# RG-LRU gates as 64x64 blocks on four array quadrants in one-bank pieces, the modulation's steps summed outside PSUM, and the keys' latent transposes ahead of the last chunk's scans

## The chip, the cores and the metric

The kernel runs on one core of one Trainium2 chip. The metric is the time of one execution in microseconds (us) as the device measures it; less is better. PE is the matrix engine (TensorE), PEld its loading of weights, DVE the vector engine, ACT the scalar engine, POOL the general-purpose engine (GpSimd), and SP the engine on whose queue all the DMAs of this kernel are issued.

## The reference, cut to what matters

The kernel computes one layer with a token mixer and a gated ConvFFN, on 1024 latent tokens and 256 context tokens of width 1024. The change touches one part of the token mixer, the RG-LRU group: 512 channels in 8 heads of 64.

```python
xr, gr, cq, ckv, kr = split_in_proj(h @ w_in)          # h: tokens, 1024 wide
xc = dwconv(xr, conv_w, conv_b, left=2)                # 4 taps
for d, reverse in ((0, False), (1, True)):             # two directions
    xh = xc.reshape(bsz, n, 8, 64)
    r = sigmoid(einsum('blhi,hij->blhj', xh, w_a[d]).reshape(bsz, n, 512) + b_a[d])
    i = sigmoid(einsum('blhi,hij->blhj', xh, w_x[d]).reshape(bsz, n, 512) + b_x[d])
    log_a = -8.0 * r * softplus(-lam[d])
    a = exp(log_a)
    u = sqrt(-expm1(2 * log_a)) * (i * xc)
    h[d] = linear_scan(a, u, h0, reverse)              # latent tokens start from the context's state
y_lru = (h[0] + h[1]) * gelu(gr)
kv = rms_norm(ckv, g_kv) @ w_ukv                       # keys and values of the attention group
```

Also in this stage is the rest of the modulation: silu(c) and silu(c_ctx) times w_mod plus b_mod gives shifts, scales and gates for later parts of the layer; some of them are worked out here.

## The kernel before

The kernel is one program whose stages follow each other. The change lies in the stage of the in-projection of the RG-LRU columns (lines 398 to 681). A loop at L656 goes over eight projections, m = 0 to 7, each 128 output channels from 1024 inputs. The first four (m < 4) are the RG-LRU's inputs over 1280 tokens (1024 latent, 256 context), in chunks of 512, 512 and 256 columns; the last four are the gate branch (Gelu) over the latent tokens alone. Each is done in split precision: weights and tokens are parted in a high and a low half (`split`, whose low half is the subtraction at L76; L69 is the copy for the high half), and three products are summed in PSUM (L492, L494, L496).

Around the projections stand three kinds of other work. "Chunk m" below is the RG-LRU work on 128 channels (two heads).

- The **modulation steps** (`mod2_step`): 16 steps of four matmuls, each on 32 of the array's columns. Four steps build up one result, which selection matmuls (L433, or L436 for the last two results) then add over groups of rows. Their weights come by DMA into two R pages per step, each step's load being issued one step ahead.
- **Conv and gates**: `conv` (L527) writes the convolved channels into a page `xc[m]`; `gate` (L540) multiplies them with a block-diagonal 128x128 matrix (two heads' 64x64 blocks, zeros elsewhere), three matmuls per gate into a three-bank PSUM tile, then one sigmoid of 1280 columns. Each chunk has four gates (two directions, r and i).
- **Coefficients and scans**: `coefs` (L558) does Exp, Tanh on ACT and a product on DVE; `scans` (L571) does Sqrt on ACT, then on DVE a multiply-add (L578), a product (L579), four scans (L581 to L587) and the sum of both directions (L591).

After projections 1, 2, 3 and 5 follow the gates, coefficients and scans of chunks 0, 1, 2 and 3. After projection 5 the tokens' other columns are also normed (`tok_norm`); `ckv_t` (L631) transposes the keys' latent part (L637) and evicts it (L642), and after projection 6 the keys' weights are loaded and split (wkh, wkl). The first matmuls that use these halves stand at L713 and L714, in the stage behind.

PSUM has here a pool with two tags: "big", two buffers of three banks (projections and gates), and "sm", two buffers of one bank (modulation steps, transposes of the keys). In SBUF the R pool has 12 pages of 128x1280, for conv, gates, coefficients and the modulation's weights; a W pool has 5 pages for weights, an L pool 30 pages. A page that is used again makes the next user wait for the last reader. A scheduler sets the order of each engine's instructions from the program's; each engine then runs its list strictly in that order, and SP issues the DMAs strictly in its order too.

Of the kernel before, what the change touches and what calls it, by code (L numbers as in the profile page):

```python
# [34 lines left out]
def hybrid_layer_kernel(ctx: ExitStack, tc: tile.TileContext, A, out):  # L35
# [20 lines left out]
    def R(dt=F32, shape=(128, 1280)):  # L56
        cnt[0] += 1
        return rp.tile(list(shape), dt, tag="R", name=f"r{cnt[0]}")
# [354 lines left out]
    def mod2_step(s):  # L413

        n, kp = divmod(s, 4)
        if s + 1 < 16:
            mod2_load(s + 1)
        if kp == 0:
            acc2[n] = ps_small()
        ws_ = w2.pop(s)  # L420
        for j in range(2):
            for h in range(2):
                g = 64 * h + 32 * j
                T.matmul(acc2[n][g:g + 32, :], cs[:, 2 * kp + j, :], ws_[j][:, h * 512:(h + 1) * 512], start=kp == 0, stop=kp == 3,
                         tile_position=(0, g))
        if kp == 3:
            mr = R()
            S.activation(mr[:, 0:512], acc2.pop(n), AF.Copy)
            po = ps_small()
            if n < 2:  # L430
                pt = po[:, 0:8].rearrange("p (m h) -> p m h", h=2)
                for m in range(4):
                    T.matmul(pt[:, m, :], mr[:, m * 128:(m + 1) * 128], sel2, start=True, stop=True)  # L433
                V.tensor_copy(mod2[:, n].rearrange("p (h m) -> p m h", h=2), pt)
            else:
                T.matmul(po[0:2, :], sel2, mr[:, 0:512], start=True, stop=True)  # L436
                r = 2 * (n - 2)
                rw, gr = (mr[0:2, 512 + 256 * x:768 + 256 * x] for x in range(2))
                for h in range(2):
                    c = slice(h * 256, (h + 1) * 256)  # L440
                    for x, q_ in ((rw, r), (gr, r + 1)):
                        nc.sync.dma_start(out=x, in_=A["rows"][q_:q_ + 1, :].rearrange("o (a b) -> (o a) b", a=2)[:, c])
                    V.tensor_tensor(rw, po[0:2, c], rw, ALU.add)
                    V.tensor_tensor(rw, rw, gr, ALU.mult)
                    nc.sync.dma_start(out=gt_d[n - 2:n - 1, :].rearrange("o (a b) -> (o a) b", a=2)[:, c], in_=rw)
# [72 lines left out]
    wg = {}  # L518

    def load_wg(m):  # L520
        wg[m] = L(F32, (128, 4, 128))
        nc.sync.dma_start(out=wg[m], in_=A["wg"][:, m * 512:(m + 1) * 512].rearrange("p (i n) -> p i n", i=4))

    SEG = ((0, SEQ), (SEQ, CTX))
    xc = {}

    def conv(m, po):  # L527

# [8 lines left out]
                V.scalar_tensor_tensor(out=x[:, a:b], in0=xr[:, a + d:b + d], scalar=cw[k], in1=x[:, a:b],  # L537
                                       op0=ALU.mult, op1=ALU.add)

    def gate(m, d, g):  # L540
        po = ps1.tile([128, 1536], F32, tag="big", name=f"pg{m}{d}{g}", bufs=2)
        for a, n in CH3:
            T.matmul(po[:, a:a + n], wg[m][:, d * 2 + g, :], xc[m][:, a:a + n], start=True, stop=True)
        r = R()
        S.activation(r, po[:, 0:NTOK], AF.Sigmoid, bias=P("bx" if g else "ba", d * 4 + m, 1))
        return r

    ysum = {}

# [3 lines left out]
        V.tensor_tensor(ysum[m], ysum[m], g[:, :SEQ], ALU.mult)  # L553

    def gates(m):
        return [(gate(m, d, 0), gate(m, d, 1)) for d in range(2)]

    def coefs(m, ri):  # L558

# [87 lines left out]
    def ps_small():  # L647
        cnt[0] += 1
        return ps1.tile([128, 512], F32, tag="sm", name=f"pm{cnt[0]}", bufs=2)
# [8 lines left out]
    for n, m in enumerate(order):  # L658
# [12 lines left out]
        if m in after:  # L671
            au = coefs(after[m], gates(after[m]))
            if m == 5:
                tok_norm()
            scans(after[m], au)
        if m == 6:
            ckv_t()
            raw = load_w(A["w_ukv"])
            wkh, wkl = prep_w(raw, "a", "v")
    pe_ctx.close()  # L680
# [1068 lines left out]
```

## Time and profile before

| what | value |
|---|---|
| time, median of 3 runs | 1319.72 us (1319.44 to 1320.05) |
| profiled execution, its own time | 1321.15 us |
| its span in the trace | 1319.3 us |
| mean granted PE clock | 0.988 of full speed |
| PE busy | 1273.5 us, 97% |
| PEld busy | 1049.8 us, 80% |
| DVE busy | 1019.7 us, 77% |
| ACT busy | 733.3 us, 56% |
| POOL busy | 410.3 us, 31% |

The busy times are shares of the span, over all stages. All times inside the trace count from the span's start. Which engine sets the time of one stage is read from that stage's own window, not from these shares.

### The profile page before, as it was taken

How to read it: one execution, taken by the hardware profiler on the slowest of the kernel's cores; microseconds unless marked ns; L12 is line 12 of the kernel's file. 1: busy time of each engine (PE TensorE's matmuls, PEld its weight loads, DVE VectorE, ACT ScalarE, POOL GpSimd, SP SyncE). 2: the span in 40 equal slices, each digit the busy share in tenths (PEclk: the TensorE clock that was granted, in tenths of full speed). 3: DMA queues.
4: the chain of work that ended last, by engine and by line, in shares of the span. 5: the costliest groups of instructions: out<-in, count | busy, mean ns of one | idle time of the engine just before them, and what ended most of it. 6: DMA issues, size and time to landing. Idle time of an engine off the chain costs nothing.

```text
span 1319.3 us, 17942 instructions
## 1 busy us (share of the span) xinstructions
PE 1273.5 (97%) x6490; PEld 1049.8 (80%) x6490; DVE 1019.7 (77%) x1654; ACT 733.3 (56%) x1374; POOL 410.3 (31%) x378
## 2 busy tenths in 40 slices
PE   5999999799999999999997999999999999999997
PEld 3796666687999999888875888888888888888885
DVE  4653676767898989857589888878777878887797
ACT  3543785557999999954265344433433444434581
POOL 2410000224666666733024433343244330000013
PEclk8999999899999999999999999999999999999998
DMA  9533234000000000243321222221222149204043
GB/s 371 201 116 128 88 127 137 24 1 1 1 1 2 1 1 24 91 159 112 128 97 55 104 81 96 96 80 64 96 96 80 64 140 356 95 0 175 1 144 127
DMA packets 41319, 124.20 MB, mean 94 GB/s; under 512 B 4600, under 2 KB 4880, under 8 KB 41232
## 3 DMA queue, kind: packets, MB, share of 16 engines
q1 hardware_dynamic: 41232, 123.07, 26.4%
q8 instruction: 51, 0.84, 0.3%
q14 instruction: 36, 0.29, 0.1%
HBM read 101.02 MB, written 22.03 MB: 93 GB/s over the span
## 4 chain that ended last, share of the span: by engine, by line
PE 80%; DVE 11%; ACT 5%; issue 2%; DMA 2%; SPq 0%; POOL 0%; DVEq 0%; ACTq 0%; POOLq 0%
PE b L1217 10%; PE b L1215 10%; PE b L1216 10%; PE t L914 5%; PE po L1063 4%; PE b L1392 4%; PE b L1391 4%; PE b L1393 4%; DVE l L76 3%; PE s L878 3%; PE o L939 3%; PE o L938 3%; PE s L879 3%; PE s L880 2%; PE po L1066 2%
## 5 line engine op out<-in xcount | busy, mean ns | idle before, releaser
L1217 PE MATMUL b<-l,f 128*128 128x512 f32 x620 | 242.6, 391 | 5.6 <-DVE f L76 5.6
L1216 PE MATMUL b<-l,f 128*128 128x512 f32 x620 | 242.9, 392 | 3.9 <-DVE l L76 3.8
L1215 PE MATMUL b<-l,f 128*128 128x512 f32 x620 | 242.4, 391 | 0.5 <-issue 0.5
L1216 PEld LDWEIGHTS b<-l,f 128*128 128x128 f32 x620 | 116.9, 189 | 30.7 <-DVE l L76 6.4
L1217 PEld LDWEIGHTS b<-l,f 128*128 128x128 f32 x620 | 117.0, 189 | 30.5 <-DVE f L76 6.4
L1215 PEld LDWEIGHTS b<-l,f 128*128 128x128 f32 x620 | 117.0, 189 | 25.1 <-issue 0.7
L1190 ACT ACTIVATE f<-w 128x1024 fp32r<-128x1024 f32 x21 | 22.3, 1060 | 198.8 <-POOL w L1187 198.8
L906 POOL TENSOR_SCALAR r<-r,c 128x512 f32<-128x512 f32 (+1 forms) x128 | 100.8, 800 | 97.3 <-DVE c L901 68.4
L883 DVE TENSOR_REDUCE c<-s 128x1 f32<-128x512 f32 (+1 forms) x192 | 108.8, 595 | 25.5 <-PE s L880 24.1
L76 DVE TENSOR_TENSOR f<-w,f 128x1024 fp32r<-128x1024 f32 (+1 forms) x90 | 98.4, 1095 | 33.8 <-ACT f L1190 32.8
L1274 DVE SCALAR_TENSOR_TENSOR l<-f,c,l 128x1023 f32<-128x1023 f32 x88 | 122.5, 1393 | 0.7
L894 ACT ACTIVATE r<-s,c 128x512 f32<-128x512 f32 (+1 forms) x192 | 117.5, 620 | 6.3 <-DVE c L901 4.8
L1184 POOL TENSOR_TENSOR w<-w 128x512 f32<-128x512 f32 x21 | 27.9, 1328 | 230.7 <-DVE f L76 230.7
L76 DVE TENSOR_TENSOR l<-t,l 128x512 fp32r<-128x512 f32 x128 | 81.5, 679 | 1.5 <-ACT l L69 1.3
L914 PE MATMUL t<-c,r 128*128 128x128 f32 x640 | 81.7, 273 | 0.9 <-DVE r L76 0.6
L1614 POOL TENSOR_TENSOR f<-f,w 128x1024 f32<-128x1024 f32 (+1 forms) x5 | 11.7, 2372 | 202.7 <-ACT l L1580 202.7
L69 ACT ACTIVATE l<-t 128x512 fp32r<-128x512 f32 x128 | 69.4, 595 | 8.5 <-PE t L914 7.7
L1268 ACT ACTIVATE l<-f,c 128x1024 f32<-128x1024 f32 x44 | 54.5, 1238 | 35.0 <-DVE f L1255 34.4
L914 PEld LDWEIGHTS t<-c,r 128*128 128x128 f32 x640 | 71.2, 140 | 2.6 <-PE t L914 0.8
L878 PE MATMUL s<-r,w 96*128 96x512 f32 (+1 forms) x192 | 69.5, 362 | 1.0 <-ACT r L894 0.7
L1063 PE MATMUL po<-l,r 128*128 128x512 f32 x256 | 69.3, 390 | 0.0
L879 PE MATMUL s<-r,w 96*128 96x512 f32 (+1 forms) x192 | 68.6, 357 | 0.0
(349 smaller groups left out, 3221.5 us busy)
## 6 DMA issues: line engine op xcount, KB each, us to landing
w<-in_w_up SPq DMA_DIRECT2D x44, 512.0 KB
r<-in_w_mod SPq DMA_DIRECT2D x32, 512.0 KB
act<-l SPq DMA_DIRECT2D x22, 512.0 KB
l<-in_w_m SPq DMA_DIRECT2D x16, 512.0 KB
l<-act SPq DMA_DIRECT2D x27, 256.0 KB
l<-in_w_dn SPq DMA_DIRECT2D x27, 256.0 KB
w<-in_w_fm SPq DMA_DIRECT2D x8, 512.0 KB
w<-in_w_out SPq DMA_DIRECT2D x8, 512.0 KB
```

The source lines that it names most:

```text
L76: return (V if e == "v" else G).tensor_tensor(o, src, f(hi), ALU.subtract)
L878: T.matmul(ps[:, :n], qh[0:96, q], kh[0:96, a:a + n], start=True, stop=False)
L879: T.matmul(ps[:, :n], qh[0:96, q], kl[0:96, a:a + n], start=False, stop=False)
L883: V.tensor_reduce(out=stat[:, i % 4, c:c + 1], in_=sc[i, c][:, :CK[c][1]], op=ALU.min, axis=AX.X)
L894: S.activation(pt_[i][:, a:a + n], sc.pop((i, c))[:, :n], AF.Exp, scale=-1.0, bias=st[:, 3:4], accum_out=st[:, 4 + c:5 + c])
L906: G.tensor_scalar(out=p[:, a:a + n], in0=p[:, a:a + n], scalar1=stat[:, i % 4, 7:8], scalar2=1.0, op0=ALU.mult, op1=ALU.mult)
L914: T.transpose(ps[:, c, :], pt_[i][:, (c0 + c) * 128:(c0 + c + 1) * 128], ident)
L1063: T.matmul(po[:, n * 512:(n + 1) * 512], w, wo[k][0][:, n * 512:(n + 1) * 512], start=st, stop=en)
L1215: T.matmul(po, wh, bh, start=k == 0 and b == wb[0][1], stop=False)
L1216: T.matmul(po, wh, bl, start=False, stop=False)
L1217: T.matmul(po, wl, bh, start=False, stop=k == 3 and b == wb[-1][1])
L1274: V.scalar_tensor_tensor(out=x[:, a], in0=x0[:, b], scalar=P("fcw", j * 3 + k, 1), in1=x[:, a], op0=ALU.mult, op1=ALU.add)
```

## The change

The gates become 64x64 blocks. `load_wg` loads only the two blocks of each gate, in four small DMAs, and lays them so that one direction's second gate has its halves swapped. `conv` also makes `xcs[m]`, a copy of the convolved channels with the two halves of partitions exchanged, by two DMAs from SBUF to SBUF. `gate_pair` takes both gates of a direction at once: for each chunk of 512, 512 and 256 columns, a **slot** of four 64x64 matmuls, one on each quadrant of the array, writes two one-bank "sm" tiles, and each is followed by a sigmoid of that chunk. So a sigmoid of 1280 columns becomes three, of 512, 512 and 256 columns, and the gates no longer use the "big" tiles.

`mod2_step` no longer sums four steps in one bank: each step takes a bank of its own, and DVE copies it into (first step) or adds it to an R page; the copy by ACT at the end goes. And `ckv_t` stands ahead of the last chunk's scans in the program.

```diff
--- before.py
+++ after.py
@@ -415,17 +415,20 @@
         n, kp = divmod(s, 4)
         if s + 1 < 16:
             mod2_load(s + 1)
-        if kp == 0:
-            acc2[n] = ps_small()
+        pm = ps_small()
         ws_ = w2.pop(s)
         for j in range(2):
             for h in range(2):
                 g = 64 * h + 32 * j
-                T.matmul(acc2[n][g:g + 32, :], cs[:, 2 * kp + j, :], ws_[j][:, h * 512:(h + 1) * 512], start=kp == 0, stop=kp == 3,
+                T.matmul(pm[g:g + 32, :], cs[:, 2 * kp + j, :], ws_[j][:, h * 512:(h + 1) * 512], start=True, stop=True,
                          tile_position=(0, g))
+        if kp == 0:
+            acc2[n] = R()
+            V.tensor_copy(acc2[n][:, 0:512], pm)
+        else:
+            V.tensor_tensor(acc2[n][:, 0:512], pm, acc2[n][:, 0:512], ALU.add)
         if kp == 3:
-            mr = R()
-            S.activation(mr[:, 0:512], acc2.pop(n), AF.Copy)
+            mr = acc2.pop(n)
             po = ps_small()
             if n < 2:
                 pt = po[:, 0:8].rearrange("p (m h) -> p m h", h=2)
@@ -518,11 +521,16 @@
     wg = {}
 
     def load_wg(m):
-        wg[m] = L(F32, (128, 4, 128))
-        nc.sync.dma_start(out=wg[m], in_=A["wg"][:, m * 512:(m + 1) * 512].rearrange("p (i n) -> p i n", i=4))
+
+        wg[m] = L(F32, (128, 2, 2, 64))
+        src = A["wg"][:, m * 512:(m + 1) * 512].rearrange("p (d g n) -> p d g n", d=2, g=2)
+        for g in range(2):
+            for b in range(2):
+                p = b ^ g
+                nc.sync.dma_start(out=wg[m][64 * p:64 * p + 64, :, g, :], in_=src[64 * b:64 * b + 64, :, g, 64 * b:64 * b + 64])
 
     SEG = ((0, SEQ), (SEQ, CTX))
-    xc = {}
+    xc, xcs = {}, {}
 
     def conv(m, po):
 
@@ -537,13 +545,23 @@
                 V.scalar_tensor_tensor(out=x[:, a:b], in0=xr[:, a + d:b + d], scalar=cw[k], in1=x[:, a:b],
                                        op0=ALU.mult, op1=ALU.add)
 
-    def gate(m, d, g):
-        po = ps1.tile([128, 1536], F32, tag="big", name=f"pg{m}{d}{g}", bufs=2)
+        y = xcs[m] = R()
+        for p in (0, 64):
+            nc.sync.dma_start(out=y[64 - p:128 - p, :], in_=x[p:p + 64, :])
+
+    def gate_pair(m, d):
+
+        ri = R(), R()
         for a, n in CH3:
-            T.matmul(po[:, a:a + n], wg[m][:, d * 2 + g, :], xc[m][:, a:a + n], start=True, stop=True)
-        r = R()
-        S.activation(r, po[:, 0:NTOK], AF.Sigmoid, bias=P("bx" if g else "ba", d * 4 + m, 1))
-        return r
+            po = [ps_small() for g in range(2)]
+            for h in (0, 64):
+                for g in range(2):
+                    o = h ^ (64 * g)
+                    T.matmul(po[g][o:o + 64, 0:n], wg[m][h:h + 64, d, g, :], (xcs if g else xc)[m][h:h + 64, a:a + n], start=True,
+                             stop=True, tile_position=(h, o))
+            for g in range(2):
+                S.activation(ri[g][:, a:a + n], po[g][:, 0:n], AF.Sigmoid, bias=P("bx" if g else "ba", d * 4 + m, 1))
+        return ri
 
     ysum = {}
 
@@ -553,7 +571,7 @@
         V.tensor_tensor(ysum[m], ysum[m], g[:, :SEQ], ALU.mult)
 
     def gates(m):
-        return [(gate(m, d, 0), gate(m, d, 1)) for d in range(2)]
+        return [gate_pair(m, d) for d in range(2)]
 
     def coefs(m, ri):
 
@@ -672,9 +690,9 @@
             au = coefs(after[m], gates(after[m]))
             if m == 5:
                 tok_norm()
+                ckv_t()
             scans(after[m], au)
         if m == 6:
-            ckv_t()
             raw = load_w(A["w_ukv"])
             wkh, wkl = prep_w(raw, "a", "v")
     pe_ctx.close()
```

Line numbers of the changed file differ: its steps' matmuls are L423, the selections L436 and L439, the gates' matmuls L560, their sigmoids L563, Exp L583, Tanh L584, Sqrt L591, the scans L599 to L605.

How the order of instructions moves is shown at three places.

**PE, the end of chunk 1's gates.** Names: pg and pm are PSUM tiles, pf a projection; r, l, w, c are pages of the pools, with their numbers. Before, the gates of chunk 1 (L543) stand among steps of the modulation (L424) and a selection (L433):

```order
L543 MATMUL pg_1277<-r_1100,l_1097 128x512
L433 MATMUL pm_1250<-c_84,r_1248 128x2 x4
L424 MATMUL pm_1260<-r_1240,c_77 32x512 x2
L424 MATMUL pm_1260<-r_1241,c_77 32x512 x2
L543 MATMUL pg_1277<-r_1100,l_1097 128x512
L543 MATMUL pg_1277<-r_1100,l_1097 128x256
L424 MATMUL pm_1260<-r_1256,c_77 32x512
L543 MATMUL pg_1283<-r_1100,l_1097 128x512 x2
L543 MATMUL pg_1283<-r_1100,l_1097 128x256
L424 MATMUL pm_1260<-r_1256,c_77 32x512
```

After:

```order
L560 MATMUL pm_1381<-r_1119,l_1113 64x256
L560 MATMUL pm_1382<-r_1128,l_1113 64x256
L560 MATMUL pm_1381<-r_1119,l_1113 64x256
L560 MATMUL pm_1382<-r_1128,l_1113 64x256
L423 MATMUL pm_1492<-r_1308,c_77 32x512 x2
L423 MATMUL pm_1492<-r_1309,c_77 32x512 x2
L423 MATMUL pm_1502<-r_1488,c_77 32x512 x2
L423 MATMUL pm_1502<-r_1489,c_77 32x512 x2
L423 MATMUL pm_1512<-r_1498,c_77 32x512 x2
L423 MATMUL pm_1512<-r_1499,c_77 32x512 x2
L439 MATMUL pm_1518<-r_1317,c_84 2x512
L560 MATMUL pm_1550<-r_1325,l_1319 64x512 x2
```

The last slot of chunk 1 is now followed by three whole steps, 9, 10 and 11, with nothing between them, then by the selection matmul that uses their sum and the first slot of chunk 2; projection 5 (pf_1699) comes after these.

**ACT, the same place.** Before, the four sigmoids of chunk 1 stand together, then the Exps and Tanhs of both directions:

```order
L545 ACT_TABLE_LOAD
L545 ACTIVATE r_1281<-pg_1277,c_70 128x1280
L545 ACTIVATE r_1287<-pg_1283,c_70 128x1280
L545 ACTIVATE r_1293<-pg_1289,c_70 128x1280
L545 ACTIVATE r_1299<-pg_1295,c_70 128x1280
L565 ACT_TABLE_LOAD
L565 ACTIVATE r_1301<-r_1281,c_851 128x1280
L565 ACTIVATE r_1305<-r_1293,c_851 128x1280
L566 ACTIVATE r_1281<-r_1281,c_852 128x1280
L566 ACTIVATE r_1293<-r_1293,c_852 128x1280
L573 ACT_TABLE_LOAD
```

After:

```order
L563 ACTIVATE r_1363<-pm_1365,c_70 128x512
L563 ACTIVATE r_1364<-pm_1366,c_70 128x512
L583 ACT_TABLE_LOAD
L583 ACTIVATE r_1389<-r_1337,c_851 128x1280
L563 ACT_TABLE_LOAD
L563 ACTIVATE r_1363<-pm_1373,c_70 128x512
L563 ACTIVATE r_1364<-pm_1374,c_70 128x512
L584 ACTIVATE r_1337<-r_1337,c_852 128x1280
L563 ACTIVATE r_1363<-pm_1381,c_70 128x256
L591 ACT_TABLE_LOAD
L591 ACTIVATE r_1337<-r_1337 128x1280
L563 ACT_TABLE_LOAD
```

The sigmoids of one direction (pages 1363 and 1364) now stand among the Exp, Tanh and Sqrt of the other (1389, 1337), with a table load at each change of function.

**SP, the loads for steps 10 and 11.** Names: w is a page for a projection's weights, r a page for the modulation's weights; the brackets list what the issue waits for (DMAHW are earlier DMAs, the others engines; the number behind a page is its buffer). Before:

```order
L411 DMA r218_1400<-in_w_mod 128x1024
L411 DMA r219_1401<-in_w_mod 128x1024 [waits DMAHW7_49,DMAHW2_49,PE_49]
L411 DMA r220_1408<-in_w_mod 128x1024 [waits DMAHW3_49,DMAHW0_49,PE_49]
L411 DMA r221_1409<-in_w_mod 128x1024 [waits DMAHW1_49,Activation_49]
L411 DMA r222_1416<-in_w_mod 128x1024 [waits DVE_49,PE_49]
L411 DMA r223_1417<-in_w_mod 128x1024 [waits DVE_49]
L442 DMA r224_1424<-in_rows 2x256 [waits DMAHW6_49,DMAHW4_49,PE_49]
L442 DMA r224_1424<-in_rows 2x256 [waits DMAHW5_49]
```

After:

```order
L480 DMA w287_1673<-in_w_fm 128x1024 [waits DMAHW5_49,DVE_49]
L550 DMA r229_1334<-r228_1325 64x1280 [waits DMAHW6_49,DVE_49]
L550 DMA r229_1334<-r228_1325 64x1280 [waits DMAHW7_49]
L480 DMA w298_1752<-in_w_fm 128x1024 [waits DMAHW5_49,DMAHW0_49,DVE_49]
L411 DMA r252_1488<-in_w_mod 128x1024 [waits DMAHW1_49,PE_49]
L411 DMA r253_1489<-in_w_mod 128x1024 [waits DMAHW2_49,PE_49]
L411 DMA r255_1498<-in_w_mod 128x1024 [waits DMAHW3_49,DVE_49,Activation_49]
L411 DMA r256_1499<-in_w_mod 128x1024 [waits DMAHW4_49,DVE_49]
L411 DMA r258_1508<-in_w_mod 128x1024 [waits DVE_49,Activation_49]
L411 DMA r259_1509<-in_w_mod 128x1024 [waits DMAHW6_49,DMAHW1_49,PE_49]
```

After the change the load of projection weights w287 waits for DVE, namely for a weight split (L76); behind it stand the two swap copies (r229 from r228, L550). Pages r252 and r253 (step 10) wait for PE's step 9, r255 and r256 (step 11) for DVE's work on chunk 1.

## Rows read from the trace of the kernel before

**Rows 1.** Page part 1: busy us, share of the span, instructions.

```profile
PE 1273.5 (97%) x6490; PEld 1049.8 (80%) x6490; DVE 1019.7 (77%) x1654; ACT 733.3 (56%) x1374; POOL 410.3 (31%) x378
```

**Rows 2.** Windows: start:end, length; PE, PEld, DVE, ACT, POOL busy; PEclk, DMA share, GB/s.

```profile
90.80:252.00 161.20, 160.75 (x733) 107.52 (x731) 100.53 (x129) 94.60 (x85) 8.74 (x5) 1.00 0.34 116
...
259.00:264.40 5.40, 5.40 (x22) 4.92 (x23) 4.61 (x6) 2.70 (x3) 0.00 (x0) 0.50 0.00 0
...
300.00:1319.00 1019.00, 996.23 (x5128) 846.71 (x5127) 832.27 (x1357) 572.21 (x1141) 367.24 (x331) 0.99 0.24 83
```

**Rows 3.** PE's waits, 80 to 320 us: us in total, times, longest.

```profile
PE ck L637 <- DVE l L642: 6.9, 1, 6.9
...
PE pm L424 <- DMA r<-in_w_mod: 0.5, 1, 0.5
```

**Rows 4.** PE's timeline: start, us, engine, line, operation, out<-in, count, [idle before].

```profile
90.77 0.75 PE L492 MATMUL pf<-l,w 128*128 128x512 f32 x3
...
104.94 2.78 PE L424 MATMUL pm<-r,c 128*32 128x512 f32 x24
...
132.41 4.56 PE L543 MATMUL pg<-r,l 128*128 128x512 f32 x12
...
191.84 0.81 PE L492 MATMUL pf<-l,w 128*128 128x512 f32 x2
...
203.03 1.90 PE L424 MATMUL pm<-r,c 128*32 128x512 f32 x10
205.39 1.05 PE L424 MATMUL pm<-r,c 128*32 128x512 f32 x4 [0.45 <-DMA r<-in_w_mod]
...
263.35 0.63 PE L714 MATMUL pb<-w,l 128*128 128x512 f32 x1
```

**Rows 5.** ACT's timeline, 147 to 184 us, columns as in rows 4.

```profile
152.13 0.60 ACT L428 ACTIVATE r<-pm 128x512 f32<-128x512 f32 x1 [0.57 <-PE pm L424]
...
155.41 1.28 ACT L545 ACT_TABLE_LOAD   x1
156.71 1.33 ACT L545 ACTIVATE r<-pg,c 128x1280 f32<-128x1280 f32 x1
...
167.85 2.62 ACT L565 ACTIVATE r<-r,c 128x1280 f32<-128x1280 f32 x2
...
178.68 1.06 ACT L69 ACTIVATE w<-w 128x1024 fp32r<-128x1024 f32 x1 [1.96 <-PE pf L494]
```

**Rows 6.** DVE's timeline, three stretches between 147 and 312 us.

```profile
147.40 2.89 DVE L578 SCALAR_TENSOR_TENSOR r<-r,r 128x1280 f32<-128x1280 f32 x2 [7.53 <-ACT r L573]
...
156.44 2.33 DVE L587 TENSOR_TENSOR_SCAN r<-r,r 128x1024 f32<-128x1024 f32 x1
...
240.23 2.89 DVE L578 SCALAR_TENSOR_TENSOR r<-r,r 128x1280 f32<-128x1280 f32 x2 [7.54 <-ACT r L573]
...
259.49 1.21 DVE L76 TENSOR_TENSOR w<-w,w 128x1024 fp32r<-128x1024 f32 x1
...
308.12 1.27 DVE L76 TENSOR_TENSOR l<-t,l 128x512 fp32r<-128x512 f32 x2
```

**Rows 7.** SP's queue, 216 to 222 us: one issue of a weight load.

```profile
217.15 0.35 SPq L477 DMA_DIRECT2D w<-in_w_fm  x1
```

**Rows 8.** Windows around that load, columns as in rows 2.

```profile
217.10:218.00 0.90, 0.90 (x11) 0.25 (x13) 0.87 (x6) 0.00 (x0) 0.00 (x0) 1.00 0.00 0
218.00:218.50 0.50, 0.50 (x12) 0.20 (x8) 0.43 (x3) 0.00 (x0) 0.00 (x0) 1.00 1.01 180
...
220.00:220.50 0.50, 0.50 (x3) 0.09 (x2) 0.00 (x0) 0.50 (x2) 0.00 (x0) 1.00 0.13 49
```

**Rows 9.** POOL's timeline, 243 to 253 us.

```profile
243.33 1.88 POOL L73 TENSOR_SCALAR l<-l 128x768 fp32r<-128x768 f32 x1 [71.03 <-PE pf L494]
...
249.52 2.08 POOL L76 TENSOR_TENSOR l<-l,l 128x768 fp32r<-128x768 f32 x1
```

## The prediction

> **What bounds the kernel now.** The page comes first: PE is busy for 1273.5 of 1319.3 us [rows 1]. The change lies in the stage of the in-projection, so I cut that stage out by windows: from 90.8 to 252.0 us PE is busy for 160.75 of 161.2 us, DVE for 100.53 and ACT for 94.60 [rows 2]. PE's own work is the length of this stage; DVE and ACT have a third to spare. The list of PE's waits adds one: 6.9 us before the transposes of the keys' latent part (L637), for DVE, which works on the last chunk's scans [rows 3]. Afterwards PE has half its clock (granted 0.50, that is 1.2 GHz) until 264.4 [rows 2]. From 300 us on PE is busy for 996 of 1019 us [rows 2], so whatever delays the first matmul that needs the low half of the keys' weights (L714, at 263.35 [rows 4]) goes to the end whole. I compare that point.
>
> **The change by its sums.** Two gates take six matmuls, 12 records, in 4.56 us [rows 4], so sixteen take 36. Now a slot is four 64x64 matmuls on four quadrants. No row shows row halves of the array at work together, but a step of the modulation is four matmuls on column quarters, and three such steps take 2.78 us [rows 4]: 0.95 for a slot of 512 columns, 0.5 for 256, 4.8 for a chunk, 19.2 for all four, if halves overlap as quarters do. The other bound, halves that take turns, doubles this (a rival below); I take the overlap, as the row of quarters is nearest. Half a step, two matmuls, costs 1.05 us [rows 4], as much as a whole one; so every step or slot that the order cuts in two pays twice. By the changed order of PE's instructions six of the 16 steps are cut (5.7), and about ten slots (some 7.7). PE's own gain is then 36 - 19.2 - 7.7 - 5.7, about 3 us.
>
> DVE gets 16 evictions of a bank, each near 0.68 (a subtraction of 128x512 out of PSUM, two in 1.27 [rows 6]): 11 us. ACT loses four copies of 0.60 and gets sigmoids in pieces: 512 columns near 0.60, 256 near 0.36, worked out between the copy's 0.60 and 1.33 for 1280 columns [rows 5]; 8 pairs cost 3.12 instead of 2.66, together 3.7 more. The changed order also holds 15 more table loads (37 against 22), 1.28 each [rows 5]: 19 us. The eight swap copies of conv's output go by DMA; they only queue on SP. By these sums nothing overflows: ACT 115, DVE 112, PE near 158. But a gate has only two banks now, and ACT must empty both before the next slot starts; so the order decides, and I walked it: each instruction gets its row's duration and starts when what it waits for is done.
>
> **The walk.** Up to the end of projection 4 there is enough projection work between the gates. Five projections (14.17 with context, 104.94 - 90.77; 11.19 without, 203.03 - 191.84 [rows 4]), nine steps, five of them cut, chunk 0's gates and chunk 1's first slot make 91 us, with 4.5 of waits: 186. Before, that projection ended at 203.0 [rows 4], with fewer gates left. Now PE has left: three projections 33.6, gates 13.45 plus 5.8 for cut slots, seven steps and a cut 7.6, two sums 1.9, transposes 1.1: 63.4, to 249.4 if it never waited. The waits:
>
> 1. Chunk 1's other five slots, with no projection between them. ACT first has to copy weights (1.06 [rows 5]) that SP may load only after DVE's weight split, which stands behind chunk 0's scans; the split ends at 187.4 in the walk. A load takes 3.1 us from issue to last byte (issued at 217.15 [rows 7]; its bytes move until just past 220 [rows 8]); ACT is free at 191.5. Then each slot is 0.95 of PE and a pair of sigmoids (1.15) in turn, and the last stands behind two table loads and an Exp (3.9 [rows 5]). PE is through at 201.6: 15.6 us for 3.85 of work, 11.75 lost.
> 2. Steps 9 to 11 of the modulation and their sum. Step 10's weights go into step 9's pages, so their load waits for step 9: 3.1 us, and 1.1 for the second. Step 11's pages come free with two DVE operations of chunk 1 (208.0 and 209.35), then 3.1 again. The sum waits for an addition that stands on DVE behind the multiply that waits for Sqrt (213.1). PE is through at 216.2: 14.6 for 3.8, 10.8 lost.
> 3. Projection 5: 1.5 lost at one slot, whose bank DVE empties late.
> 4. Chunk 2's other slots, with four short pieces of projection: 229.6 to 241.0 for 6.75 of work, 4.65 lost.
> 5. Steps 12 to 14: two more loads that wait for the step before; and projection 6 needs projection 4's banks, which ACT empties by a Gelu that stands behind four table loads, with an Exp, a Sqrt and a Tanh. 241.0 to 252.35 for 2.85, 8.5 lost.
> 6. Projections 6 and 7 with chunk 3's slots: 1.5 lost.
>
> Together 38.7, so PE ends the projections near 288, against 252.
>
> **The tail.** The transposes now stand ahead of the last scans, and their wait of 6.9 us goes. But on DVE the split of the keys' weights (L76) still stands behind these scans. The first Sqrt of chunk 3 ends at 286.7 in the walk. From the first multiply to the last scan's end DVE took 11.4 us in chunk 0 (147.40 to 156.44 + 2.33 [rows 6]); with a product, the sum of directions and the split, 1.13 each when queued (1.21 alone [rows 6]), that makes 14.8: 301.5. In the last chunk of before the scans, product and sum with two evictions of the keys' part took 4.3 us longer, 19.26 from 240.23 to 259.49 [rows 6] against 15.0 by these prices, while POOL split the queries' weights (243.33 to 251.6 [rows 9]). In the change that load waits for the last projection, so POOL's work meets the scans again, partly: between 0 and 4.3, I take 2.2. The low half is then ready at 303.7; before, its first use was at 263.35. **The sum is 40.3 us later.** The half clock after the wait is paid in both. Made against the profiled 1321.15 us this is 1361.4; against the median of the runs, 1319.72, it is 1360.
>
> **The rivals.**
>
> The walk holds: 1360, chance 0.68.
>
> Row halves take turns. Both halves of a gate write the same bank, in different partitions. A slot is then 1.9: 19.2 more, of which some 2 vanish in waits: 1377. For it: no row has row halves. Against it: column quarters, which also share one bank, do overlap [rows 4]. Chance 0.12. The Trainium skill, TensorEngine Tiling (Array Packing), section Restrictions and Gotchas, states this as a rule: different row tiles cannot access one PSUM bank at the same time. By that rule the four quadrants would give two at a time and the time would be 1377; no run here shows it yet.
>
> The loads and pages cost less than I gave them: if pages come free earlier, half of waits 2 and 5 goes (10 us), and POOL misses the scans (2): 1348. For it: before, PE waited 0.5 us in all for such loads [rows 3]; against: there the next pages were not the last step's. Chance 0.11.
>
> Faster: the slots hide behind projection work after all and PE never waits. Then PE ends at 249.4, but the tail still follows the last gates: 303.7 - 38.7 = 265, 1.6 later than before, 1321. It is faster only if cut slots cost nothing either (5.8): 1315. The point that decides: less than 4 of the 38.7 us of waits may remain. For it: ACT, DVE and PE all fit by their sums. Against: three stretches where the order puts nothing between slots or steps. Chance 0.06 (faster), and 0.03 for no change, where the waits left just eat the gain.
>
> **How the numbers follow.** 1360 is the likeliest. The range goes down past the third rival to 1342, since savings at several waits can add, and up to 1378 for the second. A change under 0.2% (2.6 us) can't be told from none. Faster 0.06, same 0.03, slower 0.91.
>
> **What would show it.** In the new trace PE's idle time between 180 and 300 should be near 40 us in three or four clumps: before gate matmuls (L560) for ACT's sigmoids (L563), before steps (L423) for loads of the modulation weights, before the sum (L439) for DVE. Table loads: 15 more. The first use of the keys' low half should come near 303, and the rest of the kernel should be as long as before. The prediction is wrong if PE stays busy through the gates, or if a slot of four takes about 1.9 us when nothing is waited for.

## The result, and the profile after

The changed kernel takes 1373.75 us (median of 4 runs, 1371.06 to 1373.80) beside 1319.88 for the kernel before in the same runs: ratio 1.0400, 95% interval 1.0382 to 1.0418, so 53.9 us slower. The prediction was 1360, with a range of 1342 to 1378. The profiled execution took 1373.77 us, with a span of 1372.0.

The page's first part, of the changed kernel (busy us, share, instructions; before: [rows 1]):

```profile
PE 1294.7 (94%) x6586; PEld 1040.0 (76%) x6586; DVE 1024.9 (75%) x1670; ACT 757.7 (55%) x1417; POOL 408.5 (30%) x378
```

PE is busy for 21 us more although the gates' matmuls do half the columns; that needs an explanation, and so do the 31 us of the longer span that are no PE work. The stage by windows (columns as in [rows 2]):

```profile
91.00:184.00 93.00, 91.29 (x458) 58.53 (x458) 39.23 (x68) 39.17 (x44) 0.64 (x1) 1.00 0.37 118
184.00:262.00 78.00, 54.54 (x213) 20.02 (x211) 39.47 (x39) 48.94 (x52) 0.00 (x0) 0.76 0.34 106
262.00:301.50 39.50, 37.57 (x166) 20.92 (x164) 24.44 (x37) 28.39 (x32) 5.33 (x4) 1.00 0.15 48
...
320.00:1372.00 1052.00, 1027.38 (x5311) 875.02 (x5309) 854.78 (x1398) 592.32 (x1182) 374.74 (x340) 0.99 0.23 81
```

Up to 184 us PE is nearly always busy, as before. From 184 to 262 it is idle for 23.5 of 78 us, and its granted clock is 0.76 on average, where before it was 1.00 in this stage. Behind 320 us nothing has changed: 1027 of 1052 us busy. From 180 to 300 us PE is idle for 25.4 us, where the prediction looked for some 40. The list of PE's waits from 80 to 345 us, its first six rows (us in total, times, longest; before: [rows 3]):

```profile
PE pm L560 <- ACT r L563: 15.6, 9, 5.2
PE pb L732 <- DVE w L76: 8.7, 1, 8.7
PE pm L423 <- DMA r<-in_w_mod: 7.3, 5, 4.2
PE pb L717 <- ACT r L570: 2.2, 1, 2.2
PE pm L423 <- ACT r L563: 1.5, 2, 1.0
PE pm L439 <- DVE r L429: 1.3, 2, 0.8
```

The clumps are those of the walk: gates for ACT's sigmoids, steps for loads, the sum (L439) for DVE, and at the end the first use of the keys' low half (L732) for DVE's split. The swap copies are not in the list: no matmul is seen to wait for one. PE's timeline in the same kernel, slots and steps picked out:

```profile
137.57 1.07 PE L560 MATMUL pm<-r,l 64*64 64x512 f32 x2
...
148.40 1.09 PE L560 MATMUL pm<-r,l 64*64 64x512 f32 x8
...
189.91 1.09 PE L560 MATMUL pm<-r,l 64*64 64x512 f32 x8
...
196.21 4.16 PE L560 MATMUL pm<-r,l 64*64 64x256 f32 x16 [5.20 <-ACT r L563]
...
206.41 1.70 PE L560 MATMUL pm<-r,l 64*64 64x256 f32 x8 [3.59 <-ACT r L563]
...
214.81 3.07 PE L423 MATMUL pm<-r,c 128*32 128x512 f32 x8 [4.24 <-DMA r<-in_w_mod]
...
220.77 1.92 PE L423 MATMUL pm<-r,c 128*32 128x512 f32 x4 [0.66 <-DMA r<-in_w_mod]
223.49 1.87 PE L439 MATMUL pm<-r,c 128*2 128x512 f32 x2 [0.79 <-DVE r L429]
...
314.99 0.80 PE L732 MATMUL pb<-w,l 128*128 128x512 f32 x1 [8.68 <-DVE w L76]
```

At 137.57 one matmul of a slot stands alone (2 records, 1.07 us), at 148.40 four on their four quadrants take 1.09. At 206.41 a slot of 256 columns takes 1.70, at 159.98 (full clock) it took 0.83; half a step (two matmuls, 4 records), 1.05 in [rows 4], takes 1.92 at 220.77. These are the same operations at the lower of the two clocks (granted 0.50), which stands behind the waits of 5.20, 3.59 and 4.24 us. The low half's first use is at 314.99, 51.6 us later than in [rows 4].

### The profile page after: what moved, and what is told of

It reads as the page before. It is cut to its first block, busy times and chain, and to the rows that moved or that the text cites. A ratio compares the mean times of both kernels' runs of the same rounds, so it can differ in the third digit from the quotient of the medians.

```text
span 1372.0 us, 18241 instructions
## 1 busy us (share of the span) xinstructions
PE 1294.7 (94%) x6586; PEld 1040.0 (76%) x6586; DVE 1024.9 (75%) x1670; ACT 757.7 (55%) x1417; POOL 408.5 (30%) x378
## 4 chain that ended last, share of the span: by engine, by line
PE 78%; DVE 11%; ACT 6%; issue 2%; DMA 2%; SPq 0%; POOL 0%; DVEq 0%; ACTq 0%; POOLq 0%
PE b L1235 9%; PE b L1233 9%; PE b L1234 9%; PE t L932 4%; PE po L1081 4%; PE b L1410 4%; PE b L1411 4%; PE b L1409 4%; DVE l L76 3%; PE s L896 3%; PE o L957 2%; PE o L956 2%; PE s L897 2%; PE s L898 2%; PE po L1084 2%
## 5 line engine op out<-in xcount | busy, mean ns | idle before, releaser
L76 DVE TENSOR_TENSOR f<-w,f 128x1024 fp32r<-128x1024 f32 (+1 forms) x90 | 98.3, 1094 | 34.6 <-ACT f L1208 33.6
L76 DVE TENSOR_TENSOR l<-t,l 128x512 fp32r<-128x512 f32 x128 | 81.5, 678 | 1.5 <-ACT l L69 1.3
L896 PE MATMUL s<-r,w 96*128 96x512 f32 (+1 forms) x192 | 69.6, 362 | 1.0 <-ACT r L912 0.7
L956 PE MATMUL o<-l,r 128*128 128x256 f32 x256 | 68.7, 301 | 0.0
```

The source lines that it names most:

```text
L76: return (V if e == "v" else G).tensor_tensor(o, src, f(hi), ALU.subtract)
L896: T.matmul(ps[:, :n], qh[0:96, q], kh[0:96, a:a + n], start=True, stop=False)
L956: T.matmul(OT[j], v, hi, start=(c == 0), stop=False)
```

## The experiments

All times are medians beside the kernel before, which took 1319.8 to 1321.1 us in these runs.

### Parts of the change alone

**Only the steps** (mod2_step as in the change's diff; gates and transposes as before).

> Of the changed kernel only the steps: each modulation step takes a bank of its own and DVE adds it into an R page; gates (128x128, one sigmoid each) and the place of the keys' transposes as before. Theory (the gates' two banks set the order): PE's work is the same, DVE gets 16 evictions of 0.68 us in a stage where it is idle for 60 us, so 1318 to 1324, PE still busy through 90 to 252. Rival (the steps' pages and evictions cost most of the 54 us): 1345 or more, with PE waiting for loads of the modulation's weights by 10 us and more.

1333.94 us, ratio 1.0105 (1.0088 to 1.0122). Neither theory's number. The loads cost little; the sum does. Its waits, and the DVE operation that ends the longest one:

```profile
PE pm L436 <- DVE r L429: 5.0, 1, 5.0
PE pm L439 <- DVE r L429: 2.8, 2, 2.6
...
PE pm L423 <- DMA r<-in_w_mod: 1.2, 1, 1.2
```

```profile
158.28 2.32 DVE L590 TENSOR_TENSOR_SCAN r<-r,r 128x1024 f32<-128x1024 f32 x1
160.53 0.66 DVE L429 TENSOR_TENSOR r<-pm,r 128x512 f32<-128x512 f32 x1
```

Before, the four steps were summed in PSUM and ACT's copy stood alone between the last step and the selection. Now the last addition (L429) stands on DVE behind the scans of chunk 0 (L590), and PE waits 5.0 us; the same once more, 2.6. PE's waits up to the low half's first use are 8.6 us longer than before, its work 3.6 us (168.6 against 165.0, the clock of the stage being 0.95 on average): together the 12.5 us by which that use comes later, within 0.3. DVE's 16 evictions fit into its idle time, but not at the place where they stand.

**Gates and steps without the moved transposes.**

```diff
             if m == 5:
                 tok_norm()
-                ckv_t()
             scans(after[m], au)
         if m == 6:
+            ckv_t()
             raw = load_w(A["w_ukv"])
```

> The changed kernel with the keys' transposes back behind projection 6, as before. Theory: the transposes' place is worth only what their wait was, and the low half of the keys' weights comes behind the scans in both; 1373 to 1380, best guess 1376. Rival (the move itself costs, since it puts three PSUM pieces into the two banks that the last gates use): faster than the changed kernel by 3 us and more, below 1370.

1373.96 us, ratio 1.0406 (1.0390 to 1.0421): the move is worth nothing here. The low half of the keys' weights comes behind the scans in both, so the wait has only another name (L655 for DVE, 14.0 us, in place of L732).

### Table loads

`last_sig` is the chunk's last sigmoid; what stands under it is issued behind it.

```diff
+            with tc.issue_after(last_sig[0].ins):
                 S.activation(a, r, AF.Exp, scale=n8[:, c])
                 S.activation(r, r, AF.Tanh, scale=p4[:, c])
```

> The changed kernel, but each chunk's Exp and Tanh are issued only after that chunk's last sigmoid, so the stage has 15 table loads fewer on ACT (19 us of ACT's time). Theory (a slot waits for two banks whatever stands between; and what follows Exp, Tanh and Sqrt comes later): 1366 to 1376, best guess 1371. Rival (the table loads between the sigmoids are the cause): 1350 to 1360.

1375.46 us, ratio 1.0415 (1.0400 to 1.0431). Fifteen table loads fewer give nothing back: PE's waits for sigmoids shrink from 15.6 to 7.5 us, those for loads (from 7.3 to 10.3) and for ACT's and DVE's other work grow.

### The swapped copy

**Without it.**

```diff
-        y = xcs[m] = R()
-        for p in (0, 64):
-            nc.sync.dma_start(out=y[64 - p:128 - p, :], in_=x[p:p + 64, :])
+        xcs[m] = x
```

> The changed kernel without the half-swapped copy: the off-diagonal quadrants read conv's own page, so their gates get the other head's channels (left out: the eight copies between partitions, with them four R pages). Theory (12 R pages are too few: loads of a step wait for the step before): a page more per chunk lets the loads of steps 10 to 14 go out early, PE's waits for modulation weights fall from 7.3 us to below 3, and with the half clock behind them 6 to 14 us come back: 1360 to 1368. Rival (pages don't matter, two gate banks do): 1371 to 1375.

1345.01 us, ratio 1.0183 (1.0167 to 1.0198): 28.7 of the 53.9 us come back, twice what the page theory allowed. What is so dear, the page, the transfers on SP's queue, or the copy between conv and gates as such? Four runs ask this.

**Page and a copy on POOL, no transfer.**

```diff
-        for p in (0, 64):
-            nc.sync.dma_start(out=y[64 - p:128 - p, :], in_=x[p:p + 64, :])
+        G.tensor_scalar(out=y, in0=x, scalar1=1.0, scalar2=1.0, op0=ALU.mult, op1=ALU.mult)
```

> The changed kernel with the second page of each chunk kept, but filled by a plain copy on POOL instead of the two swap copies by DMA (left out: the exchange of the halves, so the off-diagonal gates get the other head's channels). If the pages are what the swap costs (12 R pages, one more held through each chunk's gates): 1365 to 1375. If it is the two transfers on SP's queue, which stand ahead of weight loads and wait for conv: 1343 to 1352, as without page and copies.

1373.30 us, ratio 1.0405 (1.0389 to 1.0420).

**The transfers on POOL's queue.**

```diff
-            nc.sync.dma_start(out=y[64 - p:128 - p, :], in_=x[p:p + 64, :])
+            nc.gpsimd.dma_start(out=y[64 - p:128 - p, :], in_=x[p:p + 64, :])
```

> The changed kernel with the swap copies issued by POOL instead of SP; nothing is left out. If the pages are the cost: 1366 to 1376, as the changed kernel. If the place in SP's queue is: 1343 to 1355.

1374.53 us, ratio 1.0408 (1.0393 to 1.0424). So it isn't SP's queue: with the copies off it, or (in the run before this) with no transfer at all, nothing comes back.

**The step sums in L pages.**

```diff
-            acc2[n] = R()
+            acc2[n] = L()
```

> The changed kernel, nothing left out, but the pages into which DVE sums the steps come from the L pool instead of the R pool: the R pool has one holder less, the swap pages stay. If the count of R pages held at once is what costs: PE's waits for loads of modulation weights fall below 5 us, 1350 to 1365. If it is only the swap pages' long hold through a chunk's gates: 1368 to 1375.

1373.02 us, ratio 1.0400 (1.0384 to 1.0415). The total doesn't change, but inside something does: the projections end at 298.68 in place of 301.54, and PE's waits for loads fall from 7.3 to 5.6 us. Then PE waits 5.7 us for the eviction of the queries' latent part (L720), which stands on DVE behind the last scans, and the gain is gone.

**The page held, but no copy.**

```diff
-        y = xcs[m] = R()
-        for p in (0, 64):
-            nc.sync.dma_start(out=y[64 - p:128 - p, :], in_=x[p:p + 64, :])
+        xcs[m] = x
+        hold[m] = R()
+        G.memset(hold[m][:, 0:1], 0.0)
...
+        ri = [gate_pair(m, d) for d in range(2)]
+        G.tensor_tensor(out=hold[m][:, 0:1], in0=ri[1][1][:, NTOK - 1:NTOK], in1=hold[m][:, 0:1], op=ALU.add)
```

> The changed kernel without any swapped copy (left out: the exchange, as in the run without pages), but with an R page per chunk taken at the same place and held until the chunk's last sigmoid, by one column that POOL writes at the start and adds to at the end. Gates wait for nothing but conv. If the page held is the cost: 1365 to 1375, as with the copies. If it is the gates' wait for a copy behind conv: 1343 to 1352, as without pages. In between would share it out.

1347.28 us, ratio 1.0203 (1.0186 to 1.0220). Against the run without page (1345.01) the page costs some 2 us; against the run with a page and POOL's copy (1373.30) the copy costs 26. My page theory falls. The stage from 91 us to the end of the projections by windows, of the changed kernel, of the one without page and copy, and of the one with the page held:

```profile
91.00:301.54 210.54, 183.43 (x833) 99.47 (x832) 103.17 (x142) 116.53 (x127) 5.97 (x5) 0.91 0.32 101
```

```profile
91.00:272.07 181.07, 171.06 (x830) 96.51 (x828) 102.85 (x142) 115.78 (x127) 5.96 (x5) 1.00 0.31 102
```

```profile
91.00:275.08 184.08, 174.02 (x829) 96.81 (x827) 102.61 (x142) 112.97 (x125) 6.96 (x12) 0.99 0.30 100
```

With the copy PE has 27.1 us of idle time and 183.4 of work, without it 10.0 and 171.1, and the clock stays at 1.00 (0.99 with the page held). Where the order differs is seen at chunk 0. PE's timeline of the kernel with page and POOL's copy, and of that without either:

```profile
129.48 1.07 PE L559 MATMUL pm<-r,l 64*64 64x512 f32 x2
...
131.46 1.07 PE L559 MATMUL pm<-r,l 64*64 64x512 f32 x2
...
133.60 1.07 PE L559 MATMUL pm<-r,l 64*64 64x512 f32 x4
...
142.29 1.09 PE L559 MATMUL pm<-r,l 64*64 64x512 f32 x8
```

```profile
128.83 1.94 PE L558 MATMUL pm<-r,l 64*64 64x512 f32 x8
...
134.53 1.09 PE L558 MATMUL pm<-r,l 64*64 64x512 f32 x8
```

In the first, the two diagonal matmuls stand alone (129.48, 131.46), the off-diagonal ones, which need the copy, come together at 133.60, and projection work is put ahead of the next slot, which comes at 142.29; in the second the next slot comes at 134.53. (The 1.94 at 128.83 is no turn taken by the quadrants: one matmul starts there, the other three together 0.86 us later, right behind DVE's eviction of a step's bank.) POOL's copy itself took 1.27 us and nobody waits for it. The order has the gates later and the projections earlier, and the distance grows: chunk 1's second slot comes at 189.91 in the changed kernel, when projection 4 is over, and at 171.41 without the copy, with the end of projection 3 and all of projection 4 still there to fill the gaps.

### Quadrants without the short banks

```diff
+        w = wg[m][:, :, d * 2 + g, :]
+        for a, n, e in ((0, 512, 0), (512, 512, 1), (1024, 256, 0)):
+            for h in (0, 64):
+                o = 64 - h if e else h
+                T.matmul(po[o:o + 64, a:a + n], w[h:h + 64, e, :], (xcs if e else xc)[m][h:h + 64, a:a + n], start=True, stop=True,
+                         tile_position=(h, o))
         r = R()
         S.activation(r, po[:, 0:NTOK], AF.Sigmoid, bias=P("bx" if g else "ba", d * 4 + m, 1))
```

Here `po` is the three-bank tile of before; each gate's weights are loaded in both arrangements.

> The kernel before with only its gates changed: each gate keeps its three-bank tile and its one sigmoid of 1280 columns, but the first 512 columns go through the diagonal quadrants and the next 512 through the off-diagonal ones at the same time, from the half-swapped copy; steps, their bank and the transposes as before. PE's work on gates falls by 40 per cent, some 14 us. If the short banks and steps are the trouble of the change, and quadrants are not: 1305 to 1318. If the swapped page costs what it costs in the changed kernel, whatever the tiles: 1325 to 1345.

1314.02 us, ratio 0.9953 (0.9938 to 0.9967): 0.5 per cent less than the kernel before, with the swap copies in it. PE's timeline, two gates in a row, and the window up to the end of the projections:

```profile
131.90 2.80 PE L554 MATMUL pg<-r,l 64*64 64x512 f32 x24
```

```profile
90.80:245.50 154.70, 151.50 (x831) 99.28 (x829) 101.09 (x129) 94.11 (x85) 8.37 (x5) 1.00 0.46 141
```

Two gates take 2.80 us in place of the 4.56 of [rows 4], eight times: 14 us less by that row; PE's busy time in the stage falls by 9.3, and 2.7 of that is lost again to idle time (a wait of 2.4 for a load of modulation weights, before 0.5). With three banks per gate and PSUM still summing the steps, the loss of the changed kernel doesn't come; what the copy costs here was not measured, since no run leaves it out of this kernel. Behind the projections PE still waits 6.5 us for the transposes' eviction, as in [rows 3].

### The tail

**Before, with the transposes ahead of the last scans, and these behind the split of the keys' weights.**

```diff
             if m == 5:
                 tok_norm()
-            scans(after[m], au)
+                ckv_t()
+            if m != 5:
+                scans(after[m], au)
         if m == 6:
-            ckv_t()
             raw = load_w(A["w_ukv"])
             wkh, wkl = prep_w(raw, "a", "v")
+            scans(3, au)
```

> The kernel before with the keys' transposes ahead of the last chunk's scans, as in the change, and these scans behind the split of the keys' weights in the program. By the profile of before the 6.9 us wait and the half clock behind it go: the first use of the low half comes near 256 instead of 263.35, 1310 to 1316. Rival (scans that come later hold R pages and DVE for the stage behind): 1320 or more.

1320.49 us, ratio 0.9996 (0.9987 to 1.0006): no change. The low half's first use comes at 254.24, 9 us sooner, and then PE waits again:

```profile
PE pb L715 <- DVE l L704: 6.1, 1, 6.1
```

```profile
261.68 2.47 DVE L704 SCALAR_TENSOR_TENSOR l<-pb,c,l 128x1024 fp32r<-128x1024 f32 x2
```

The next DVE work that PE needs, the eviction of the queries' latent part (L704), stands behind the same scans. The wait moved by one operation.

**The same with the quadrant gates in three-bank tiles** (the last two diffs together).

> Quadrant gates in three-bank tiles (the kernel that took 1314.0) with the keys' transposes ahead of the last scans and these scans behind the split of the keys' weights in the program. There the gates are done some 7 us sooner, so the scans end near 250, about when the evictions of the queries' latent part are due: the wait of 6.5 us shrinks to 1 or 2 and the half clock behind it goes: 1306 to 1311. Rival (the wait only moves behind the scans, as it did with gates of before): 1313 to 1315.

1313.57 us, ratio 0.9952 (0.9935 to 0.9968): as without the move. The rival was right: a wait of 5.6 us for L716, the same eviction, takes the place of the 6.5.

**And the split of the queries' weights behind the values.** The block that loads and splits w_uq moves down:

```diff
-    wuq = []
-    for k in range(2):
-        raw = L(F32, (128, 768))
...
     for p in range(5):
         values(p)
+    wuq = []
+    for k in range(2):
+        raw = L(F32, (128, 768))
...
     keys(0)
```

> As the quadrant gates in three-bank tiles with transposes and keys' split ahead of the last scans, and besides the load and split of the queries' weights (POOL, 7.7 us) behind the values in the program, so that POOL doesn't work while DVE scans. In the kernel before, a scan of 256 columns took 2.32 us beside POOL, 0.68 alone; so DVE is through the scans some 4 us sooner: 1303 to 1309. Rival (POOL's split is then late for the queries): 1312 or more.

1319.36 us, ratio 0.9996 (0.9986 to 1.0005): the gain of the quadrants is gone. The split is late for the queries:

```profile
PE pb L758 <- DVE r L789: 4.5, 1, 4.5
PE pb L720 <- DVE l L709: 4.0, 1, 4.0
...
PE pb L759 <- POOL l L76: 1.6, 1, 1.6
```

PE now waits 4.0 us for the eviction (5.6 in the run before), 4.5 for DVE's L789 (1.0), and 1.6 for POOL's split itself. But the order lost time earlier too. At 200 us the wait for a step's weights is 2.55 us in place of 2.00, and the clock behind it is lower. Windows of the run before and of this one:

```profile
200.00:215.00 15.00, 15.00 (x72) 9.62 (x68) 12.52 (x22) 1.43 (x2) 0.00 (x0) 1.00 0.37 127
```

```profile
200.00:215.00 15.00, 14.03 (x48) 10.06 (x49) 13.45 (x23) 0.90 (x1) 0.00 (x0) 0.77 0.31 111
```

The projections end at 249.58 in place of 245.07. So of the 8.4 us by which this profiled execution (1321.70, the longest of ten, the shortest 1318.06) has the longer span, 4.5 are lost before the split is needed; how much of the median's 5.8 us is the late split is not shown.

## Why the prediction was right, and where it was off

**The direction and the mechanism.** The walk named the point at which the time is decided, the first use of the keys' low half, and its mechanism: the work fits, but the order leaves stretches with nothing between slots and steps. The point came 51.6 us later (263.35 to 314.99), against 40.3 worked out; the span grew by 52.7, so the rest of the kernel was as long as before within 1.1 us. The sums of ACT (115) and DVE (112) were near or too large: from 91 us to the end of the projections they worked for 116.5 and 103.2. PE's sum was not right.

**The milestones.** Projection 4 ended at 189.9 (walk 186), chunk 1's slots at 208.1 (201.6), the sum behind steps 9 to 11 at 225.4 (216.2), chunk 2's slots at 251.2 (241.0), steps 12 to 14 at 262.4 (252.35), the projections at 301.5 (288). The clumps lie where they were put, and nearly all took longer than in the walk; but not because of longer waits.

**The sizes: PE's work too small, its waits too large.** Up to the end of the projections the walk held 154.4 us of PE's work (91 and 63.4) and 43.2 of waits (4.5 and 38.7). The changed kernel had 183.4 and 27.1. The work was 29.0 too small, the waits 16.1 too large, and only the difference, 12.9, shows in the end of the projections. That 1360 came so near is in part luck: with waits of the true size and work as priced it would have been 1344. Two terms of the work were mis-sized.

One is the price of slots and steps in pieces, 19.2 and 7.7 for the slots, 15.2 and 5.7 for the steps: 26.9 and 20.9. By groups (line, engine, operation, count; busy us, mean ns; idle before), of the kernel before, of the changed one, of the one without the copy, where the clock stayed at 1.00, and of the one with quadrants in three-bank tiles:

```profile
L543 PE MATMUL pg<-r,l 128*128 128x512 f32 (+1 forms) x96 | 38.0, 535 | 0.0
L424 PE MATMUL pm<-r,c 128*32 128x512 f32 x128 | 20.0, 601 | 0.5 <-DMA r<-in_w_mod 0.5
```

```profile
L560 PE MATMUL pm<-r,l 64*64 64x512 f32 (+1 forms) x192 | 39.0, 593 | 15.9 <-ACT r L563 15.6
L423 PE MATMUL pm<-r,c 128*32 128x512 f32 x128 | 33.5, 762 | 9.4 <-DMA r<-in_w_mod 7.3 <-ACT r L563 1.5 <-ACT r L591 0.6
```

```profile
L558 PE MATMUL pm<-r,l 64*64 64x512 f32 (+1 forms) x192 | 37.4, 544 | 5.6 <-ACT r L561 4.7 <-DVE r L446 0.4
L423 PE MATMUL pm<-r,c 128*32 128x512 f32 x128 | 23.7, 602 | 2.1 <-DMA r<-in_w_mod 2.0
```

```profile
L554 PE MATMUL pg<-r,l 64*64 64x512 f32 (+1 forms) x192 | 26.5, 534 | 0.0
```

At the full clock the slots took 37.4 us, 10.5 more than priced and no less than the gates before, and the steps 23.7, 2.8 more: in the changed order the four matmuls of a slot seldom stand all together, and one alone or two cost as much as four (1.07 to 1.09, above). In the three-bank tiles, where they do stand together (24 records in 2.80 us), the quadrants save 11.5 us of the 38.0. These lines also explain the 21 us by which PE is busier: in the changed kernel the gates save nothing (38.0 to 39.0), the steps take 13.5 us more, and the three products of the projections, cut into more pieces, some 7.

The other is the clock inside the gaps. The sum priced the half clock only behind the tail's wait ("paid in both"). But the gaps of 5.20, 3.59 and 4.24 us at chunk 1 end with a granted clock of 0.50, behind the one of 3.16 us at chunk 2 it falls too, and slots and steps then take 1.8 to 2 times as long. Against the kernel without the copy the steps took 9.8 us more, the slots 1.6, the selections 0.9 (2.9 against 2.0): 12.3 in all. The prediction's sums gave PE 158 us in this stage (its walk 154.4); without the copy it worked for 171.1, with it for 183.4.

The half clock alone is not what the walk lacked, though its 12.3 us are near the 13.5 at the end of the projections: 3.9 of these were lost before 189.9 and 3.5 behind 262.4, at a granted clock of 1.00, and 6.1 between. The 12.3 come from comparing two kernels whose orders differ, not from a run in which the clock alone changed.

**Row halves overlap.** The second rival gave a slot 1.9 us; four matmuls took 1.09, one alone 1.07 (above), and in the three-bank tiles twelve took 2.80. The prediction's 0.95 was worked out from steps that follow each other; standing alone, 1.09 is the price. The Trainium skill, TensorEngine Tiling (Array Packing), section Restrictions and Gotchas, has different row tiles kept from one bank; here both row tiles write one bank, in different partitions, and the rows show no turn taken. For this use the measurement decides.

**The swap copies, priced at nothing.** The prediction said they "only queue on SP". SP's queue is indeed not where they cost, nor, but for some 2 us, the page; but leaving them out gives 28.7 us back. The walk held much of this cost without naming it, since it followed the changed kernel's order, copies and all. Of the 53.9 us then about 26 come with the copy, 13 were measured for the steps alone, and the rest, some 15, is left to the two short banks and what the parts do to each other. That the three add up was not tried, and no run has the gates in short banks with the steps as before. Without the copy the stage is still 20 us longer than before, 10.4 of it more work of PE (171.1 against 160.6) and 9.6 more idle time.

**Pages and loads (waits 2 and 5, third rival).** The waits for loads of modulation weights are there (7.3 us, before 0.5), but the reading that the R pages are too few is not borne out: step sums in L pages end the projections 2.9 us sooner and leave the total as it was, and the held page costs 2 us.

**The tail.** From the first multiply to the low half I had 14.8 us, plus 2.2 for POOL beside the scans. DVE's and POOL's timelines of the changed kernel:

```profile
300.18 2.89 DVE L596 SCALAR_TENSOR_TENSOR r<-r,r 128x1280 f32<-128x1280 f32 x2 [2.10 <-ACT r L591]
...
313.72 1.22 DVE L76 TENSOR_TENSOR w<-w,w 128x1024 fp32r<-128x1024 f32 x1
```

```profile
297.97 1.85 POOL L76 TENSOR_TENSOR l<-l,l 128x768 fp32r<-128x768 f32 x1
```

From 300.18 to the split's end at 314.94 it is 14.8. POOL ended at 299.8, before the scans began, so the 2.2 were not due. The transposes' place gained nothing, as the sum had it.

**Open.** Why a copy that takes 1.27 us on POOL, and for which no engine is seen to wait, leads to an order with the gates 8 us later at chunk 0, lies in the scheduler's rules, which no profile shows. Only the orders and their times are shown. An order fixed by hand with the copies and the short banks was not tried, so that the order itself is the cause is argued from the timelines, not shown by a run.

## What to carry to other kernels

Work that fits by the sums of every engine can still be lost in the order: walk the stretch, and ask what the engine has left to do in each gap when its filler is used up early. Hold the walk's work and its waits against the trace one by one: here both were wrong, in opposite directions, and the sum hid it. Work that comes in pieces is to be priced by the piece. A producer put between two steps is priced not by its duration or its queue but by what the order does with everything behind it; take it out once and measure. And a wait that is removed in front of a busy engine is worth only the distance to the next operation that is queued behind the same work: here the low half came 9 us sooner and the kernel took as long as before, since the next eviction stood behind the same scans.

## What the runs showed that was not expected

- Quadrants pay when the tiles and the steps stay as before: 40% of the gates' columns saved are worth 6.7 us (1314.02 against 1320.67) even with eight swap copies.
- A wait of 5.2 us inside a stage that PE had filled until then ends with a granted clock of 0.50 (1.2 GHz), while waits of up to 2.3 us in the kernel without the copy left the stage's mean at 1.00. In the last of the tail's runs a wait of 2.55 us was followed by a lower clock (0.77 on average over 15 us). Windows of the changed kernel around 196.21:

```profile
188.00:192.00 4.00, 3.00 (x17) 1.52 (x15) 3.58 (x6) 0.00 (x0) 0.00 (x0) 1.00 0.06 11
192.00:196.00 4.00, 0.00 (x0) 0.00 (x0) 0.39 (x1) 1.48 (x2) 0.00 (x0) 0.67 0.96 281
196.00:200.00 4.00, 3.79 (x16) 1.16 (x16) 2.33 (x2) 1.68 (x4) 0.00 (x0) 0.50 0.39 134
```
- A scan of 256 columns took 2.32 us while POOL split weights, 0.68 when it didn't. In the kernel before, chunk 0, without POOL, and then in the kernel with quadrants in three-bank tiles, DVE and POOL:

```profile
153.02 0.68 DVE L581 TENSOR_TENSOR_SCAN r<-r,r 128x256 f32<-128x256 f32 x1
```

```profile
239.58 2.32 DVE L593 TENSOR_TENSOR_SCAN r<-r,r 128x256 f32<-128x256 f32 x1
...
238.40 2.96 POOL L76 TENSOR_TENSOR l<-l,l 128x768 fp32r<-128x768 f32 x1
```

The Trainium skill, SBUF — State Buffer, section SBUF: two separate sides, has DVE and GpSimd share a pair of ports by exclusive lock. The rows agree in kind: the scan ends 0.54 us behind POOL's operation of 2.96 (241.90 and 241.36) and took 1.6 us longer than alone.
